# Dilated attention scores: the order of the 128-column and the 32-column matmuls within a visit

## The chip, the cores and the metric

The kernel runs on one core of a Trainium2 chip. The metric is the device time of one execution in microseconds (us), as the median of several runs. TensorE (PE in the profile) multiplies matrices, VectorE is DVE, ScalarE is ACT, GpSimd is POOL, and SyncE (SP) issues most transfers.

## The reference

The program is a trunk of two layers over 512 tokens of width 1024. The first layer mixes tokens by attention in three groups of windows: group 0 is local, group 1 looks at every fourth token, group 2 at every sixteenth. Each group has 16 heads of 64, and the three results are merged by their softmax denominators. The second layer is a gated linear attention. A SwiGLU follows each. Only the scores of the two dilated groups matter here; cut down they are:

```python
A_GROUPS = ((128, 1), (512, 4), (2048, 16))     # window, dilation
half = window // (2 * dilation)
...
scores = jnp.einsum("nbqhd,nbkhd->nbhqk", qp, kb) * (dh ** -0.5)
scores = jnp.where(valid, scores, NEG_INF)
m = jnp.max(scores, axis=-1, keepdims=True)
p = jnp.exp(scores - m)
l = jnp.sum(p, axis=-1)
o = jnp.einsum("nbhqk,nbkhd->nbqhd", p, vb)
```

With 512 tokens, a phase of group 1 has 128 tokens and a phase of group 2 has 32. So 128 queries of one token block need a 128x128 score matrix for group 1, and four 32x32 squares for group 2.

## The kernel before, in words

Nearly all of PE's time goes to projections in split precision: a float32 weight is split into a high and a low part (`wh` by ACT at L107, `wl` by DVE at L108), the activations as well, and three matmuls of 512 columns stand for one product. In the attention layer `chunk_of` (L639) makes these projections; its three matmuls are L658, L659 and L660, and they write the PSUM tiles `ppp`.

`attend_dilated(u)` (L826) does the two dilated groups for four heads (u is 0 to 3): a chunk of keys, one of values, one of queries, and then four **visits**. A visit takes one pair of heads (`pr`) and two of the four token blocks (`i0`, `i0+1`). It has these steps:

- Scores on PE, in float32. Each head of the pair (`a` is 0 or 1) has its own PSUM tile, `pss[a]`, named `ps` in the profile; a block `b` takes 160 columns of it. Columns 0 to 127 are group 1, one matmul of 64 rows by 128 columns per head and block (L851). Columns 128 to 159 are group 2, four matmuls of 64 rows by 32 columns (L856), here called the pieces. Head 0 lies in rows 0 to 63 of the array and head 1 in rows 64 to 127; a piece writes only 32 partitions, so it uses a quarter of the columns. A float32 matmul stands twice in the trace, as two passes, each with its own weight load: 256 pieces in the program are 512 records.
- Softmax (L738): on DVE a masked minimum for each head and block (L748, tile `sm`), on ACT the exponential (L749).
- Turning (L752): four transposes on PE (L757), a copy by ACT (L782), and for the pieces DVE transposes and a spread (L785, L787).
- Weighing (L797): PE multiplies the turned weights with the values into `po`. It is held back by one visit (`self.pending`): the weights of visit n are used behind the transposes of visit n+1.

There are 4 times 4 visits. A scheduler places their instructions among the projections of the chunk that follows, so that between the scores of a visit and its transposes PE works on L658 to L660. Each engine then runs its own instructions in that fixed order. The two score tiles of a visit reuse the two PSUM buffers of the visit before (`"s": 2` in `PBUFS`), which are free once ACT has copied them (L782). In the second visit of u = 0 the scheduler placed the first matmuls of the two heads apart, as the order below shows. After the dilated visits, from about 380 us on, come the local visits with scores in L891.

Of the kernel before, what the change touches and what calls it, by code (L numbers as in the profile page):

```python
# [4 lines left out]

# [1 line left out]

# [15 lines left out]
P = 128  # L23
# [5 lines left out]
HD = 64  # L29
# [12 lines left out]
class Trunk:  # L42
# [300 lines left out]
    def product(self, acc, x, w, width, start, apart=False):  # L343
        mm = self.nc.tensor.matmul
        per = 1024 // width
        last = KT // 2 - 1
        def high(i, k, wh):
            f = slice(k % per * width, (k % per + 1) * width)
            for x_part, first in zip(x[k], (start and k == 0, False)):
                mm(acc[i][:, 0:width], lhsT=x_part[:, i * P:(i + 1) * P], rhs=wh[:, f], start=first, stop=False,  # L350
                   skip_group_check=True)

        def low(i, k, wl):
            f = slice(k % per * width, (k % per + 1) * width)
            self.multiplied = mm(acc[i][:, 0:width], lhsT=x[k][0][:, i * P:(i + 1) * P], rhs=wl[:, f], start=False,  # L355
                                 stop=k == last, skip_group_check=True)

        for n, (wh, wl) in enumerate(w):
            ks = range(n * per, n * per + per)
            for group in ((0,), (1,)) if apart or n == len(w) - 1 else ((0, 1),):  # L360
                for i in group:
                    for k in ks:
                        high(i, k, wh)
                for i in group:
                    for k in ks:
                        low(i, k, wl)
# [459 lines left out]
    def attend_dilated(self, u):  # L826
        nc = self.nc
        k = self.qk_chunk("k", u)
        v = self.v_chunk(self.ins["a_w_v"][u], 0)
        q1, q = self.qk_chunk("q", u)  # L830
        st = self.t("st", (P, NT, 2, 4))
        o_dram = []

        def store(pr, po):
            ob = self.t("ob", (P, 4, 4, 32))
            nc.vector.transpose(ob.rearrange("q r p j -> q p r j"), po.rearrange("q (p r s) -> q p r s", p=4, r=4))
            od = self.dr.tile([S * P], F32, name=f"o_dram_{u}_{pr}")
            for a in range(4):
                nc.gpsimd.dma_start(od.rearrange("(s t a d) -> a s t d", s=32, a=4, d=32)[a],
                                    ob[32 * a:32 * a + 32].rearrange("s r p j -> s (r p) j"))  # L840
            o_dram.append(od)

        for pr in range(2):
            for i0 in (0, 2):
                pss = [self.p("s") for _ in range(2)]
                for b in range(2):
                    i = i0 + b
                    tok = slice(i * P, (i + 1) * P)
                    for a in range(2):
                        r = slice(a * HD, (a + 1) * HD)  # L850
                        nc.tensor.matmul(pss[a][:, b * 160:b * 160 + P], lhsT=q1[pr][r, tok], rhs=k[r, pr, :, i],  # L851
                                         start=True, stop=True)
                    for g in range(4):
                        for a in range(2):
                            r = slice(a * HD, (a + 1) * HD)
                            nc.tensor.matmul(pss[a][32 * g:32 * g + 32, b * 160 + P:b * 160 + 160],  # L856
                                             lhsT=q[r, 2 + pr, g, i], rhs=k[r, 2 + pr, g, i], start=True, stop=True)
                sms = []
                for a in range(2):
                    stats = [[st[:, i0 + b, s, 2 * pr + a:2 * pr + a + 1] for s in range(2)] for b in range(2)]  # L860
                    sms.append(self.softmax(pss[a], [(0, 160)] * 2, 160, self.masks[:, 0:160], stats))
                pts = self.turned(pss, sms, 2, 160, self.finish_dilated)
                vals = lambda i, c, f: v[i][:, c * 256 + f:c * 256 + f + HD]
                self.pending = pts, vals, pr * P, i0, partial(store, pr) if i0 == 2 else None
        std = self.dr.tile([S * 8], F32, name=f"st_dram_{u}")
        for r in range(4):
            nc.gpsimd.dma_start(std.rearrange("(s r c) -> r s c", r=4, c=32)[r],
                                st[32 * r:32 * r + 32].rearrange("p a b c -> p (a b c)"))
        return o_dram, std
# [499 lines left out]
```

## Time and profile before

| what | value |
|---|---|
| median of 3 runs | 1441.89 us (1441.7 to 1441.99) |
| the profiled execution, its own time | 1441.3 us |
| its span in the profile | 1439.5 us |
| PE busy | 1434.3 us (100%) |
| DVE busy | 1019.7 us (71%) |
| ACT busy | 745.8 us (52%) |
| granted clock of PE over the run | 1.0 |

A row of the timeline has the start in us from the span's start, the length in us, the engine, the line of the kernel, the operation, the tiles written and read, the shape, the number of merged records, and in brackets the idle time before it with what ended it. The length of a merged row goes from the first record's start to the last one's end. PE records overlap, because a matmul starts in the array while the one before still drains, so PE is measured here by the time from one start to the next start.

### The profile page before, as it was taken

Reading aid. Unit: us, or ns where it says so; the run is one execution under the profiler, and the core shown is the slowest. Engines: PE = TensorE matmul, PEld = TensorE weight load, DVE = VectorE, ACT = ScalarE, POOL = GpSimd, SP = SyncE. Lnnn points to the kernel's source line nnn. Section 1 sums busy time; section 2 is a strip of 40 time slices with the busy share of each in tenths; the row PEclk is TensorE's granted clock in tenths of the full one; section 3 lists DMA queues with packets and bytes.
Section 4 is the critical chain, followed back from the end, with each engine's and each line's share of the span. In section 5 each row is a group of like instructions: output and inputs, shape, how many; then the busy total and the mean of one; then the engine's idle time right before and its main releaser. Section 6 shows DMA issues by size and latency. Waiting matters only on the chain.

```text
span 1439.5 us, 21062 instructions
## 1 busy us (share of the span) xinstructions
PE 1434.3 (100%) x7766; PEld 1191.0 (83%) x7766; DVE 1019.7 (71%) x1862; ACT 745.8 (52%) x1274; POOL 170.6 (12%) x270
## 2 busy tenths in 40 slices
PE   9999999999999999999999999999999999999999
PEld 8887878787888888888888887888888888889887
DVE  6685868778689669887786335757576987779322
ACT  6444444545456647655575224555744755557211
POOL 0001020101322212211130000000010222221000
PEclk9999999999999999999999999999999999999999
DMA  8544344464543438777785333212155887776542
GB/s 276 140 132 110 104 119 118 101 189 107 132 137 103 122 113 235 194 215 221 230 211 183 122 114 105 88 45 88 56 172 168 231 222 215 214 188 187 169 129 70
DMA packets 96104, 218.57 MB, mean 152 GB/s; under 512 B 15200, under 2 KB 38560, under 8 KB 96000
## 3 DMA queue, kind: packets, MB, share of 16 engines
q1 hardware_dynamic: 78768, 164.62, 35.6%
q0 software_dynamic: 17088, 52.58, 16.6%
q8 instruction: 61, 1.00, 0.3%
q14 instruction: 43, 0.35, 0.1%
q10 hardware_dynamic: 144, 0.02, 0.0%
HBM read 184.59 MB, written 19.99 MB: 142 GB/s over the span
## 4 chain that ended last, share of the span: by engine, by line
PE 94%; DVE 4%; ACT 1%; issue 1%; DMA 0%; DVEq 0%; SPq 0%
PE ppp L121 19%; PE ppp L350 14%; PE ppp L123 10%; PE ppp L660 9%; PE ppp L659 9%; PE ppp L658 9%; PE ppp L355 7%; PE ps L350 6%; PE ps L355 3%; PE po L797 2%; PE ps L851 1%; PE ps L757 1%; PE ppp L1195 1%; PE ps L891 1%; ACT sm L749 1%
## 5 line engine op out<-in xcount | busy, mean ns | idle before, releaser
L107 ACT ACTIVATE wh<-wf 128x1024 fp32r<-128x1024 f32 (+1 forms) x200 | 208.2, 1042 | 325.6 <-PE ppp L121 185.0
L108 DVE TENSOR_TENSOR wl<-wf,wh 128x1024 fp32r<-128x1024 f32 (+1 forms) x200 | 239.3, 1197 | 184.5 <-ACT wh L107 184.1
L658 PE MATMUL ppp<-wh,xs 128*128 128x512 f32 (+1 forms) x668 | 255.3, 382 | 0.0
L660 PE MATMUL ppp<-wh,xs 128*128 128x512 f32 (+1 forms) x668 | 254.5, 381 | 0.0
L659 PE MATMUL ppp<-wl,xs 128*128 128x512 f32 (+1 forms) x668 | 254.3, 381 | 0.0
L121 PE MATMUL ppp<-xs,wh 128*128 128x512 f32 x544 | 170.3, 393 | 0.0
L658 PEld LDWEIGHTS ppp<-wh,xs 128*128 128x128 f32 x668 | 125.6, 188 | 26.9 <-issue 3.4
L660 PEld LDWEIGHTS ppp<-wh,xs 128*128 128x128 f32 x668 | 125.6, 188 | 24.0 <-issue 0.3
L659 PEld LDWEIGHTS ppp<-wl,xs 128*128 128x128 f32 x668 | 125.6, 188 | 23.7 <-issue 0.2
L107 ACT ACTIVATE wh<-wA 128x1024 fp32r<-128x1024 f32 x88 | 93.3, 1061 | 98.1 <-PE ppp L350 37.7
L350 PE MATMUL ppp<-wh,a 128*128 128x512 f32 (+1 forms) x576 | 139.4, 373 | 0.0
L121 PEld LDWEIGHTS ppp<-xs,wh 128*128 128x128 f32 x544 | 101.4, 188 | 23.4 <-issue 1.5
L108 DVE TENSOR_TENSOR wl<-wA,wh 128x1024 fp32r<-128x1024 f32 x88 | 107.3, 1219 | 16.6 <-ACT wh L107 16.6
L350 PEld LDWEIGHTS ppp<-wh,a 128*128 128x128 f32 x576 | 102.1, 188 | 20.0 <-ACT g L415 1.5
L123 PE MATMUL ppp<-xs,wl 128*128 128x512 f32 x272 | 106.0, 390 | 0.0
L749 ACT ACTIVATE sm<-sm,st 128x160 f32<-128x160 f32 (+2 forms) x128 | 56.8, 446 | 45.4 <-DVE st L748 45.2
L355 PE MATMUL ppp<-wl,a 128*128 128x512 f32 (+1 forms) x288 | 78.4, 371 | 0.0
L269 POOL DMA_DIRECT2D wA<-in_gate_up_dram x44 | 38.5, 882 | 312.6 <-DVE wl L108 256.7
L350 PE MATMUL ps<-wh,sh 128*128 128x512 f32 (+1 forms) x192 | 70.3, 371 | 0.0
L350 PE MATMUL ps<-wh,sl 128*128 128x512 f32 (+1 forms) x192 | 70.3, 371 | 0.0
L350 PE MATMUL ppp<-wh,sh 128*128 128x512 f32 (+1 forms) x192 | 70.3, 371 | 0.0
L350 PE MATMUL ppp<-wh,sl 128*128 128x512 f32 (+1 forms) x192 | 70.3, 371 | 0.0
(317 smaller groups left out, 2619.3 us busy)
## 6 DMA issues: line engine op xcount, KB each, us to landing
wA<-in_gate_up_dram POOLq DMA_DIRECT2D x52, 512.0 KB, 6.0
wf<-in_gate_up_dram SPq DMA_DIRECT2D x40, 512.0 KB, 5.1
wf<-in_down_dram SPq DMA_DIRECT2D x32, 512.0 KB, 3.7
wf<-in_a_w_v_dram SPq DMA_DIRECT2D x20, 512.0 KB, 3.7
turned<-g POOLq DMA_DIRECT2D x80, 128.0 KB, 7.4
zq<-zs SPq DMA_DIRECT2D x152, 64.0 KB, 2.1
wf<-in_a_w_q_dram SPq DMA_DIRECT2D x16, 512.0 KB, 3.8
wf<-in_a_w_qk_dram SPq DMA_DIRECT2D x16, 512.0 KB, 3.9
```

The source lines that it names most:

```text
L107: nc.scalar.activation(hi, src, AF.Copy)
L108: self.low = nc.vector.tensor_sub(lo, src, hi.bitcast(F32))
L121: mm(out, lhsT=wh, rhs=part, start=start and k + n == 0, stop=False)
L123: self.multiplied = mm(out, lhsT=wl, rhs=x[0], start=False, stop=stop and k == len(w) - 1)
L269: self.added = nc.gpsimd.dma_start(raw[tag][i], dram[block, i], accum_op=ALU.add)
L350: mm(acc[i][:, 0:width], lhsT=x_part[:, i * P:(i + 1) * P], rhs=wh[:, f], start=first, stop=False, skip_group_check=True)
L355: self.multiplied = mm(acc[i][:, 0:width], lhsT=x[k][0][:, i * P:(i + 1) * P], rhs=wl[:, f], start=False, stop=k == last, skip_group_check ...
L658: mm(a, lhsT=xh, rhs=wh[:, f], start=k == 0, stop=False)
L659: mm(a, lhsT=xh, rhs=wl[:, f], start=False, stop=False)
L660: self.multiplied = mm(a, lhsT=xl, rhs=wh[:, f], start=False, stop=k == KT - 1)
L749: nc.scalar.activation(sm[:, w], sm[:, w], AF.Exp, bias=n, scale=-1.0, accum_out=l)
L797: self.nc.tensor.matmul(o, lhsT=vals(i0 + b, c, c0 + a * HD), rhs=pts[a][b][c], start=c == 0, stop=c == 1)
```

## The change

In a visit the loops over block, head and piece are taken apart: first the four 128-column matmuls of both blocks, then the sixteen pieces of both blocks. The products, operands, PSUM tiles and columns stay the same. Four lines go, so that L851 becomes L848, L856 becomes L852, and all later lines move up by four.

```diff
-from itertools import chain
+from itertools import chain, product
...
                 pss = [self.p("s") for _ in range(2)]
-                for b in range(2):
-                    i = i0 + b
-                    tok = slice(i * P, (i + 1) * P)
-                    for a in range(2):
-                        r = slice(a * HD, (a + 1) * HD)
-                        nc.tensor.matmul(pss[a][:, b * 160:b * 160 + P], lhsT=q1[pr][r, tok], rhs=k[r, pr, :, i],
-                                         start=True, stop=True)
-                    for g in range(4):
-                        for a in range(2):
-                            r = slice(a * HD, (a + 1) * HD)
-                            nc.tensor.matmul(pss[a][32 * g:32 * g + 32, b * 160 + P:b * 160 + 160],
-                                             lhsT=q[r, 2 + pr, g, i], rhs=k[r, 2 + pr, g, i], start=True, stop=True)
+                for b, a in product(range(2), range(2)):
+                    r, i = slice(a * HD, (a + 1) * HD), i0 + b
+                    nc.tensor.matmul(pss[a][:, b * 160:b * 160 + P], lhsT=q1[pr][r, i * P:(i + 1) * P],
+                                     rhs=k[r, pr, :, i], start=True, stop=True)
+                for b, g, a in product(range(2), range(4), range(2)):
+                    r, i = slice(a * HD, (a + 1) * HD), i0 + b
+                    nc.tensor.matmul(pss[a][32 * g:32 * g + 32, b * 160 + P:b * 160 + 160],
+                                     lhsT=q[r, 2 + pr, g, i], rhs=k[r, 2 + pr, g, i], start=True, stop=True)
```

The order of DVE, ACT, POOL and SP is the same in both programs. On PE, this is the first visit of u = 0 before the change. `ps_787` and `ps_788` are the score tiles of the two heads, `zq_429` holds the keys, `qk_782` the queries of group 1, `zq_765` those of group 2.

```order
L658 MATMUL ppp_1223<-wh_1287,xs_151 128x512
L851 MATMUL ps_787<-zq_429,qk_782 128x128
L851 MATMUL ps_788<-zq_429,qk_782 128x128
L856 MATMUL ps_787<-zq_429,zq_765 32x32
L856 MATMUL ps_788<-zq_429,zq_765 32x32
...
L851 MATMUL ps_787<-zq_429,qk_782 128x128
L851 MATMUL ps_788<-zq_429,qk_782 128x128
```

And the same place after it:

```order
L658 MATMUL ppp_1223<-wh_1287,xs_151 128x512
L848 MATMUL ps_787<-zq_429,qk_782 128x128
L848 MATMUL ps_788<-zq_429,qk_782 128x128
L848 MATMUL ps_787<-zq_429,qk_782 128x128
L848 MATMUL ps_788<-zq_429,qk_782 128x128
L852 MATMUL ps_787<-zq_429,zq_765 32x32
L852 MATMUL ps_788<-zq_429,zq_765 32x32
```

The two 128-column matmuls of the second block moved ahead of the eight pieces of the first; the sixteen pieces now stand in one row, and the projection L659 follows as before. Fifteen of the sixteen visits have this pattern.

The second visit of u = 0 is the other one. On PE before, with `ps_835` and `ps_836` as the tiles of the two heads:

```order
L658 MATMUL ppp_1222<-wh_1317,xs_163 128x512
L851 MATMUL ps_835<-zq_429,qk_782 128x128
L856 MATMUL ps_835<-zq_429,zq_765 32x32
L851 MATMUL ps_836<-zq_429,qk_782 128x128
L856 MATMUL ps_836<-zq_429,zq_765 32x32
```

And after:

```order
L658 MATMUL ppp_1222<-wh_1317,xs_163 128x512
L848 MATMUL ps_835<-zq_429,qk_782 128x128 x2
L848 MATMUL ps_836<-zq_429,qk_782 128x128 x2
L852 MATMUL ps_835<-zq_429,zq_765 32x32
L852 MATMUL ps_836<-zq_429,zq_765 32x32
```

Here one piece of head 0 stood between the 128-column matmuls of the two heads. Now both blocks of head 0 come first, then both of head 1, and all pieces behind them.

## The prediction, on record before the run

> **What bounds the kernel now.** I read the page first, then the waits of PE, then the timeline of PE at the dilated visits, then DVE and ACT at the places where a visit's softmax is late.
>
> ```profile
> span 1439.5 us, 21062 instructions
> PE 1434.3 (100%) x7766; PEld 1191.0 (83%) x7766; DVE 1019.7 (71%) x1862; ACT 745.8 (52%) x1274; POOL 170.6 (12%) x270
> PE 94%; DVE 4%; ACT 1%; issue 1%; DMA 0%; DVEq 0%; SPq 0%
> ```
>
> PE is busy for 1434.3 of 1439.5 us, and the chain that ended last is PE for 94%. All the waits of PE in the whole run are these:
>
> ```profile
> PE ppp L92 <- DVE acc L89: 1.2, 1, 1.2
> PE ppp L651 <- DVE wh L105: 0.5, 1, 0.5
> PE pt L818 <- DVE ob L926: 0.2, 1, 0.2
> ```
>
> So time taken out of PE's row ends the program earlier, as long as no wait grows in its place. The change touches PE alone, at the sixteen dilated visits. This is the first one, in PE's timeline:
>
> ```profile
> 106.44 0.39 PE L658 MATMUL ppp<-wh,xs 128*128 128x512 f32 x1
> 106.76 0.49 PE L851 MATMUL ps<-zq,qk 64*128 64x128 f32 x4
> 107.18 0.29 PE L856 MATMUL ps<-zq,zq 64*32 64x32 f32 x16
> 107.40 0.49 PE L851 MATMUL ps<-zq,qk 64*128 64x128 f32 x4
> 107.83 0.29 PE L856 MATMUL ps<-zq,zq 64*32 64x32 f32 x16
> 108.05 0.50 PE L659 MATMUL ppp<-wl,xs 128*128 128x512 f32 x1
> ```
>
> From start to start a visit is 0.42 + 0.22 + 0.43 + 0.22 = 1.29 us: four phases, and nothing idle between them.
>
> **The change part by part.** *The 128-column phase.* What does one pass cost when passes follow each other, and what does a phase cost for standing alone? The transposes have 128 columns as well, and the local scores have two blocks in one phase, with the same halves of the array:
>
> ```profile
> 110.93 0.60 PE L757 MATMUL ps<-ident,sm 128*128 128x128 f32 x4
> L757 PE MATMUL ps<-ident,sm 128*128 128x128 f32 x64 | 9.7, 274 | 0.0
> 380.40 1.03 PE L891 MATMUL ps<-zq 64*128 64x192 f32 x8
> 381.36 0.50 PE L658 MATMUL ppp<-wh,xs 128*128 128x512 f32 x1
> ```
>
> Four transpose records last 0.60 us, and one lasts 0.274, so their starts lie (0.60 - 0.274) / 3 = 0.109 apart. A phase of L851 is two such passes, since the two heads run side by side: 0.218 us. It takes 0.42, so standing alone costs it 0.20: its first weight load, which nothing covers, and the emptying of the array before the next shape. L891 has two blocks, of 192 and 256 columns. At 0.109 us per 128 columns its four passes are 2 x 0.163 + 2 x 0.218 = 0.76 us; with 0.20 once that is 0.96, with 0.20 for each block 1.16. The row says 381.36 - 380.40 = 0.96. So blocks of one shape in a row pay the 0.20 once. Merged, the phase is 0.42 + 0.22 = 0.64 us where two took 0.85: 0.20 saved.
>
> *The piece phase.* How long one piece lasts is in the records of that line:
>
> ```profile
> L856 PE MATMUL ps<-zq,zq x512: 192/203/213, 107.2 to 359.1; 64*32 64x32 f32 x171
> ```
>
> The sixteen records (eight pieces, two passes) last 0.29 us, the last of them 0.192, so the last starts 0.10 behind the first: 0.0066 us each, 0.106 for sixteen. The phase takes 0.22, so 0.116 is the cost of standing alone. Merged it is 0.22 + 0.106 = 0.328 us instead of 0.44: 0.116 saved, if sixteen more starts go as fast as the first sixteen. At worst they pay as much as a phase by itself or more; that is the second and third rival. The Trainium skill ("TensorE: Matmul & The Clock Gate", the section "Wait — 56ns, not 53.3ns?") states that start-to-start never falls below about 25 ns, however few the columns. The 6.6 ns here, where eight tiles of the array work side by side, do not agree with it; by that rule the sixteen added starts would take 0.40 us and the piece phase 0.62.
>
> An ordinary visit so goes from 1.29 to 0.64 + 0.33 = 0.97 us, 0.32 saved, and fifteen of them save 4.8 us.
>
> *The odd visit*, the second of u = 0:
>
> ```profile
> 112.16 0.48 PE L851 MATMUL ps<-zq,qk 64*128 64x128 f32 x2
> 112.57 0.24 PE L856 MATMUL ps<-zq,zq 64*32 64x32 f32 x2
> 112.75 0.48 PE L851 MATMUL ps<-zq,qk 64*128 64x128 f32 x2
> 113.16 0.28 PE L856 MATMUL ps<-zq,zq 64*32 64x32 f32 x14
> 113.38 0.49 PE L851 MATMUL ps<-zq,qk 64*128 64x128 f32 x4
> 114.02 0.50 PE L659 MATMUL ppp<-wl,xs 128*128 128x512 f32 x1
> ```
>
> It has six phases and takes 114.02 - 112.16 = 1.86 us. With two phases it is 0.97, and 0.89 is saved, if the two heads still run side by side although head 1 now stands behind both blocks of head 0. If not, four more passes of 0.109 follow each other, it takes 1.41, and 0.45 is saved. I take 0.89: the lone piece above lasts 0.24, so its second pass starts 0.05 behind its first, yet sixteen records start within 0.10. PE must therefore be starting other tiles while one waits for its second pass.
>
> PE's row gets shorter by 4.8 + 0.89 = 5.7 us.
>
> *What is given back.* Nothing on DVE, ACT, POOL or SP is added or moved, and no queue is passed; transfers are issued behind the same instructions. Scores of both heads are complete at the end of the visit in either order, so the softmax starts no later than now in relation to PE. But where DVE is late for its own reasons, the softmax does not come earlier by the visit's own 0.32 us, while the transposes do. The fourth visit of u = 1 shows it:
>
> ```profile
> 196.28 0.32 DVE L748 CUSTOM_DVE_ANT_0 sm<-ps,masks 128x160 f32<-128x160 f32 x1 [0.16 <-PE ps L856]
> 201.60 0.29 PE L856 MATMUL ps<-zq,zq 64*32 64x32 f32 x16
> 202.73 0.32 DVE L748 CUSTOM_DVE_ANT_0 sm<-ps,masks 128x160 f32<-128x160 f32 x1
> 204.73 0.19 ACT L749 ACTIVATION_READ_ACCUMULATOR sm<-sm,st 128x1 f32 x1
> 205.38 0.60 PE L757 MATMUL ps<-ident,sm 128*128 128x128 f32 x4
> ```
>
> PE's scores end at 201.89, DVE turns to them at 202.73, ACT is through at 204.92, and the transposes start at 205.38: 0.46 us to spare. DVE last waited for PE at 196.28, by 0.16. If DVE's work since the first visit of the group moves by 0.32 + 0.16 = 0.48 only, and PE by four visits, 1.28, then 1.28 - 0.48 - 0.46 = 0.34 us come back as a wait. The fourth visits of u = 0 and u = 2 have less to spare:
>
> ```profile
> 124.51 0.72 DVE L836 STREAM_TRANSPOSE ob<-po 128x512 f32<-128x512 f32 x1 [0.53 <-PE po L797]
> 128.25 0.19 ACT L749 ACTIVATION_READ_ACCUMULATOR sm<-sm,st 128x1 f32 x1
> 128.55 0.49 PE L757 MATMUL ps<-ident,sm 128*128 128x128 f32 x3
> 283.10 0.47 PEld L757 LDWEIGHTS ps<-ident,sm 128*128 128x128 f32 x4 [0.15 <-ACT sm L749]
> ```
>
> In the first DVE waited for PE just ahead of the visit (0.53 at 124.51), so only the visit's own 0.32 counts, against 128.55 - 128.44 = 0.11 to spare: some 0.2 us back. In the second the weight load already waits 0.15 for ACT: up to 0.3 back. At u = 3 a low weight part comes close:
>
> ```profile
> 352.44 1.22 DVE L108 TENSOR_TENSOR wl<-wf,wh 128x1024 fp32r<-128x1024 f32 x1
> 353.96 0.39 PE L659 MATMUL ppp<-wl,xs 128*128 128x512 f32 x1
> ```
>
> It is done at 353.66 and needed at 353.96, 0.30 to spare against 0.32: 0.1 back there, with other small ones. The sum is 0.34 + 0.2 + 0.3 + 0.2 for the rest, about 1.1 us; from both sides it is 0 (all of DVE moves with PE) and, if DVE stood still over each group, up to the first rival's 4.7. I take 1.1, because the waits above are seen. Behind the groups DVE has room, so nothing adds up:
>
> ```profile
> DVE wl L108 <- ACT wh L107: 10.2, 2, 5.9
> ```
>
> This is DVE's wait between 363 and 380 us, 10.2 us of it, ahead of the local visits.
>
> The sum: 5.7 - 1.1 = 4.6 us. The profiled execution took 1441.3 us, 1.8 more than its span, and would take 1436.7. The median of the runs shown is 0.6 above it, 1441.9, so I forecast 1437.3 us. About 0.2% (2.9 us) is what a measurement of this kernel can tell from no change.
>
> **Rivals.** *First: the softmax does not come along.* DVE and ACT stay where they are within each group of four visits, and the transposes wait. To spare are 0.1, 0.46, 0.1 and 0.05 us or so, against 1.85, 1.28, 1.28 and 0.96, so 1.75 + 0.8 + 1.2 + 0.9 = 4.7 of the 5.7 us would come back, and the time is 1440.9. For it: DVE is late in the fourth visits. Against it: DVE's brackets above show it waiting for PE in every group, so its work starts earlier as well. A chance of 0.08 for most of this.
>
> *Second: the pieces are fed slowly.* How many matmuls stand ready for PE when the phase begins? The semaphore waits of PE's sequencer tell where it is:
>
> ```profile
> L851 PEldq EVENT_SEMAPHORE  x2: 51/51/51, 104.4 to 104.5; - x2
> L856 PEldq EVENT_SEMAPHORE  x4: 51/51/51, 104.7 to 105.0; - x4
> L856 PEldq EVENT_SEMAPHORE  x2: 51/51/51, 106.8 to 107.0; - x2
> ```
>
> Each of the first eight pieces of this visit has one such wait. When the scores begin at 106.76, the sequencer is at the seventh: it runs ahead by two L851 and six pieces, about eight matmuls, and stops there until some leave. Before the change eight pieces are a whole phase. Now, of sixteen, eight must be fed while the others run. Call the time to feed one f. The phase is then 8 f + 0.05 for the last second pass + 0.12 to the next phase, 8 f + 0.17, as soon as that is over 0.328. From the rows: four pieces with their waits take 0.1 each (104.7 to 105.0), and two waits with nothing between them are 0.1 apart too (104.4 to 104.5), which leaves a piece nearly nothing; so I take f at 0.02 and the phase at 0.33. At most f is 0.09: by 107.93 the sequencer has delivered ten more matmuls (two L851, eight pieces) since 107.0. If f is 0.05, two starts of 25 ns, the phase takes 0.57 and a visit 1.21 instead of 1.29; sixteen save 1.3, with the odd visit's further 0.57 some 1.8 us, and the time is 1440.1, no change that can be told. This is also what the Trainium skill's floor would make of the pieces that are not queued. A chance of 0.11.
>
> *Third, on the other side: they are fed at the upper bound.* With f = 0.09 the piece phase takes 0.89 and a visit 1.53 instead of 1.29: sixteen lose 3.9, the odd visit gives 0.6 back, and the time is 1445.2. It turns at f = 0.06, where 0.64 + 8 f + 0.17 is 1.29. For it: nothing before the change has more than eight pieces in a row. Against it: the row at 104.4 to 105.0. A chance of 0.05.
>
> *Fourth: the merged phase still empties between blocks*, and the change does nothing: 1441.9. L891 speaks against it. A chance of 0.04.
>
> **How the numbers follow.** My forecast, from 1436.0 (nothing given back, 1441.9 - 5.7, rounded) to about 1438.9 (0.45 for the odd visit, 2.3 given back), has 0.72. The rest of the range up to 1440.0 holds milder forms of the first two rivals. Left out are the end of the second, the third, the fourth and the full first: 0.2. So the range is 1436.0 to 1440.0. Faster by over 0.2%, below 1439.0: 0.72 and a few hundredths of mild forms, 0.75. Within 0.2%: 0.20. Slower: 0.05.
>
> **What would show it.** In the changed profile a visit should have two phases: L848 x8 with 0.64 us to the first L852, and L852 x32 with 0.33 to the next line; the odd visit too. Records of L852 that start further apart in the second half than in the first would show the second or third rival. New waits of PE at L757 for ACT `sm` L749, in the fourth visits above all, would show what is given back. The prediction is wrong if the L848 phase takes 0.85, if the L852 phase takes over 0.5, or if PE's waits in the four groups add up to over 2.5 us.

## The result, and the profile after

The changed kernel takes 1436.85 us, the median of 5 runs (1436.51 to 1436.94); the kernel before took 1441.89 us in 5 runs (1441.7 to 1442.41). The ratio is 0.9964, with a 95% interval of 0.9951 to 0.9976: 5.0 us less, where 4.6 were forecast (1437.3 us, range 1436.0 to 1440.0). The profiled execution took 1436.52 us. Its page:

```profile
span 1434.7 us, 21062 instructions
PE 1429.4 (100%) x7766; PEld 1188.2 (83%) x7766; DVE 1018.6 (71%) x1862; ACT 746.0 (52%) x1274; POOL 170.9 (12%) x270
```

The span is 4.8 us shorter, PE's busy time 4.9 and that of its weight loads (PEld) 2.8; no other engine's changed by more than about 1 us. All the waits of PE that the trace lists:

```profile
PE ppp L92 <- DVE acc L89: 1.2, 1, 1.2
PE ppp L659 <- DVE wl L108: 0.2, 1, 0.2
PE pt L818 <- DVE ob L922: 0.2, 1, 0.2
PE ppp L651 <- DVE wh L105: 0.2, 1, 0.2
```

Only the second is new, and it has nothing to do with the visits: it ends at 8.58 us, at the program's start. Between 100 and 400 us the list has no wait at all. The first visit in PE's timeline, and then the second one, the odd one before the change:

```profile
107.40 0.71 PE L848 MATMUL ps<-zq,qk 64*128 64x128 f32 x8
108.05 0.36 PE L852 MATMUL ps<-zq,zq 64*32 64x32 f32 x32
108.33 0.50 PE L659 MATMUL ppp<-wl,xs 128*128 128x512 f32 x1
...
112.41 0.72 PE L848 MATMUL ps<-zq,qk 64*128 64x128 f32 x8
113.06 0.35 PE L852 MATMUL ps<-zq,zq 64*32 64x32 f32 x32
113.34 0.50 PE L659 MATMUL ppp<-wl,xs 128*128 128x512 f32 x1
```

From start to start a visit is now 0.65 + 0.28 = 0.93 us where it was 1.29, and the odd visit is 0.93 where it was 1.86. All sixteen visits have two phases; one of them, the fourth of u = 1, takes 0.98 because its first phase is 0.69 long. To see what became of that time over the whole stretch, compare the projection that follows the last visit, in PE's timeline of before and then of after:

```profile
359.20 0.50 PE L660 MATMUL ppp<-wh,xs 128*128 128x512 f32 x1
```

```profile
354.43 0.50 PE L660 MATMUL ppp<-wh,xs 128*128 128x512 f32 x1
```

From the start of the first visit to the end of the last it was 359.20 - 106.76 = 252.44 us and is 354.43 - 107.40 = 247.03: 5.41 less. Added over the sixteen visits, the time from the first score matmul to the next other line fell from 21.16 to 14.93 us, 6.23 less. So 0.82 us came back as waits between the visits. Behind the last visit nothing changed: 1439.5 - 359.20 = 1080.3 before, 1434.7 - 354.43 = 1080.3 after. The first visit starts 0.64 us later in this profile; that lies ahead of all that the change touches, and nearly all of it arises at the wait that ends at 8.58 us: L658 ahead of it starts at 7.84 us before and 7.85 after, L660 behind it at 8.30 and 8.92. In the profiles of the experiments that leave the first visit where it was, it starts between 107.2 and 108.0 us. So the difference of the two spans is 5.41 - 0.64 = 4.8 us.

Where did the 0.82 us come back? Normally a transpose starts 0.23 us behind the start of the projection ahead of it. In the fourth visits it does not; here are those of u = 0, 1 and 2 in PE's timeline, then the low weight part of u = 3:

```profile
127.01 0.39 PE L659 MATMUL ppp<-wl,xs 128*128 128x512 f32 x1
127.52 0.65 PE L757 MATMUL ps<-ident,sm 128*128 128x128 f32 x4
...
202.72 0.39 PE L659 MATMUL ppp<-wl,xs 128*128 128x512 f32 x1
203.10 0.44 PE L757 MATMUL ps<-ident,sm 128*128 128x128 f32 x2
...
279.27 0.39 PE L660 MATMUL ppp<-wh,xs 128*128 128x512 f32 x1
279.74 0.44 PE L757 MATMUL ps<-ident,sm 128*128 128x128 f32 x2
...
349.19 0.40 PE L658 MATMUL ppp<-wh,xs 128*128 128x512 f32 x1
349.54 0.50 PE L659 MATMUL ppp<-wl,xs 128*128 128x512 f32 x1
349.88 0.40 PE L660 MATMUL ppp<-wh,xs 128*128 128x512 f32 x1
```

The starts lie 0.51, 0.38 and 0.47 apart, so 0.28, 0.15 and 0.24 us are lost; at u = 3, behind the third visit, it is twice about 0.11, where L659 starts late, at 349.54, just behind the end of a low weight part on DVE (349.49). That makes 0.9 us. Against it, the transposes of one visit of u = 3 were 0.07 late before the change and no longer are, which leaves the 0.82 within 0.02. PE's list of waits does not name any of these; the times from start to start show them. Why the softmax is late shows on DVE at the fourth visit of u = 0:

```profile
124.18 1.18 DVE L108 TENSOR_TENSOR wl<-wf,wh 128x1024 fp32r<-128x1024 f32 x1
125.28 0.31 DVE L748 CUSTOM_DVE_ANT_0 sm<-ps,masks 128x160 f32<-128x160 f32 x1
```

The visit's scores started at 123.41 and are complete at 124.41, but DVE is inside a low weight part and turns to them at 125.28.

### The profile page after: what moved, and what is told of

Read it like the earlier page. It is cut to its first block, busy times and chain, and to the rows that moved or that the text cites. A ratio compares the mean times of both kernels' runs of the same rounds, so it can differ in the third digit from the quotient of the medians.

```text
span 1434.7 us, 21062 instructions
## 1 busy us (share of the span) xinstructions
PE 1429.4 (100%) x7766; PEld 1188.2 (83%) x7766; DVE 1018.6 (71%) x1862; ACT 746.0 (52%) x1274; POOL 170.9 (12%) x270
## 4 chain that ended last, share of the span: by engine, by line
PE 91%; DVE 6%; ACT 2%; issue 1%; DMA 0%; SPq 0%; DVEq 0%; ACTq 0%
PE ppp L121 19%; PE ppp L350 14%; PE ppp L123 10%; PE ppp L660 8%; PE ppp L659 8%; PE ppp L658 8%; PE ppp L355 7%; PE ps L350 6%; PE ps L355 3%; PE po L797 1%; ACT sm L749 1%; DVE wl L108 1%; PE ps L757 1%; PE ppp L1191 1%; DVE sm L748 1%
## 5 line engine op out<-in xcount | busy, mean ns | idle before, releaser
L108 DVE TENSOR_TENSOR wl<-wf,wh 128x1024 fp32r<-128x1024 f32 (+1 forms) x200 | 239.2, 1197 | 188.8 <-ACT wh L107 188.4
L658 PE MATMUL ppp<-wh,xs 128*128 128x512 f32 (+1 forms) x668 | 255.7, 383 | 0.0
L659 PE MATMUL ppp<-wl,xs 128*128 128x512 f32 (+1 forms) x668 | 254.7, 381 | 0.2 <-DVE wl L108 0.2
L660 PE MATMUL ppp<-wh,xs 128*128 128x512 f32 (+1 forms) x668 | 254.8, 381 | 0.0
L658 PEld LDWEIGHTS ppp<-wh,xs 128*128 128x128 f32 x668 | 125.7, 188 | 27.0 <-issue 3.3
L659 PEld LDWEIGHTS ppp<-wl,xs 128*128 128x128 f32 x668 | 125.7, 188 | 24.3 <-DVE wl L108 0.9
L660 PEld LDWEIGHTS ppp<-wh,xs 128*128 128x128 f32 x668 | 125.7, 188 | 23.9 <-issue 0.3
L108 DVE TENSOR_TENSOR wl<-wA,wh 128x1024 fp32r<-128x1024 f32 x88 | 107.4, 1220 | 16.6 <-ACT wh L107 16.6
```

The lines of the kernel that those rows point to most:

```text
L108: self.low = nc.vector.tensor_sub(lo, src, hi.bitcast(F32))
L658: mm(a, lhsT=xh, rhs=wh[:, f], start=k == 0, stop=False)
L659: mm(a, lhsT=xh, rhs=wl[:, f], start=False, stop=False)
L660: self.multiplied = mm(a, lhsT=xl, rhs=wh[:, f], start=False, stop=k == KT - 1)
```

## The experiments

The theory was: (1) what is saved is the cost of a change of shape, about 0.20 us for each 128-column phase and 0.16 for each piece phase (0.222 alone, of which 0.063 stay when it is merged), so the number of phases sets the visit's time, and the order within them does not matter; (2) sixteen pieces go in a row without being fed slowly; (3) what is given back comes from DVE's low weight part ahead of the fourth visits' softmax. The rivals were that the heads' adjacency or the place of a phase counts, that the pieces run dry, and that the waits come from elsewhere. Five of the kernels split a visit into two functions, and differ in one line:

```diff
+                def wide(b):
+                    for a in range(2):
+                        ...
+                def pieces(b):
+                    for g, a in product(range(4), range(2)):
+                        ...
+                for step, b in (...):
+                    step(b)
```

### Only the 128-column phases merged

```diff
+                for step, b in ((pieces, 0), (wide, 0), (wide, 1), (pieces, 1)):
```

> Order of a visit: pieces of block 0, the 128-column matmuls of both blocks, pieces of block 1 (three phases instead of before's four; the second visit of u = 0 has five). Theory (each phase pays once for its first weight load and for the emptying of the array): an ordinary visit takes 0.222 + 0.645 + 0.222 = 1.09 us instead of 1.29, 15 visits save 3.0 us, the odd one some 0.4, about 0.5 comes back in waits: about 1439.0 us (1438.4 to 1439.8), and the middle phase is 0.645 long. Rival (what counts is that the 128-column matmuls stand ahead of all pieces, for the softmax behind them): the gain is gone, about 1442.

Measured: 1451.49 us (1451.32 to 1451.74), ratio 1.0066 [1.0053, 1.008]. The visit came out as expected and the total did not. An ordinary visit:

```profile
120.85 0.29 PE L855 MATMUL ps<-zq,zq 64*32 64x32 f32 x16
121.07 0.71 PE L849 MATMUL ps<-zq,qk 64*128 64x128 f32 x8
121.72 0.29 PE L855 MATMUL ps<-zq,zq 64*32 64x32 f32 x16
121.94 0.50 PE L660 MATMUL ppp<-wh,xs 128*128 128x512 f32 x1
```

That is 0.22 + 0.65 + 0.22 = 1.09 us: the merged 128-column phase costs the same here, between two piece phases, as in the changed kernel. The total is lost elsewhere. Since the pieces now stand first, the scheduler places the first visit's pieces one by one between projections, eight in each of the four groups. One of them:

```profile
98.53 0.40 PE L658 MATMUL ppp<-wh,xs 128*128 128x512 f32 x1
98.86 0.24 PE L855 MATMUL ps<-zq,zq 64*32 64x32 f32 x2
99.03 0.50 PE L659 MATMUL ppp<-wl,xs 128*128 128x512 f32 x1
99.38 0.40 PE L660 MATMUL ppp<-wh,xs 128*128 128x512 f32 x1
```

From 98.53 to 99.38 it is 0.85 us, where two projections take 0.46: one lone piece costs 0.39 us. Thirty-two of them are 12.5, less 0.9 for the four piece phases that they replace and 3.2 for the merged phases: 8.4 of the 9.7 us that this kernel is slower; the rest was not traced. The odd visit was expected to save 0.4 and saves 0.2: it has five phases and takes 1.67 us. The visits' phases decide on the theory here, the total does not.

### Only the piece phases merged

```diff
+                for step, b in ((wide, 0), (pieces, 0), (pieces, 1), (wide, 1)):
```

> Order of a visit: 128-column matmuls of block 0, the sixteen pieces of both blocks, 128-column matmuls of block 1 (three phases in all sixteen visits). Theory (cost per phase): a visit takes 0.422 + 0.285 + 0.422 = 1.13 us instead of 1.29, 15 visits save 2.4 us, the odd one 0.7, about 0.5 comes back: about 1439.3 us (1438.6 to 1440.0). Rival (the 128-column matmuls must stand first): about 1442.

Measured: 1441.92 us (1441.49 to 1442.74), ratio 1.0 [0.9991, 1.001], beside 1441.76 of before. Again the phases are as expected. An ordinary visit, and then a projection at 317 us:

```profile
118.38 0.49 PE L849 MATMUL ps<-zq,qk 64*128 64x128 f32 x4
118.81 0.35 PE L855 MATMUL ps<-zq,zq 64*32 64x32 f32 x32
119.09 0.49 PE L849 MATMUL ps<-zq,qk 64*128 64x128 f32 x4
119.51 0.50 PE L660 MATMUL ppp<-wh,xs 128*128 128x512 f32 x1
...
317.12 0.50 PE L658 MATMUL ppp<-wh,xs 128*128 128x512 f32 x1 [1.18 <-ACT xs L151]
```

Three phases take 0.43 + 0.28 + 0.42 = 1.13 us, and the merged piece phase costs the same 0.28 between two 128-column phases. Over all visits this takes 2.6 us out of PE's row, although the first phases of three visits are some 0.5 us longer. Yet the time did not fall. The reordered scores led the scheduler to another order on DVE, ACT and SP, and with it came the wait of 1.18 us for ACT at 317 us; from start to start PE loses about 2.0 us between 312 and 326 us. From the start of the first visit to the end of the last it is 252.14 us, 0.3 less than before; this profile also started about 1 us late. So the total says nothing about the phases.

### All pieces first

```diff
+                for step, b in ((pieces, 0), (pieces, 1), (wide, 0), (wide, 1)):
```

> Order of a visit: all sixteen pieces first, then the four 128-column matmuls; in the first visit of each u the scheduler puts the 128-column matmuls between the pieces of the two blocks. Theory (cost per phase): twelve visits have two phases and take 0.93 us as in the changed kernel, four have three and take 1.09, so 0.6 us more than the changed kernel: about 1437.5 us (1436.8 to 1438.2). Rival (the 128-column matmuls must stand first): 1441 or more.

Measured: 1449.98 us (1449.45 to 1450.86), ratio 1.0056 [1.0043, 1.007]. An ordinary visit is two phases with the time of the changed kernel, 0.29 + 0.64 = 0.93 us:

```profile
120.60 0.36 PE L855 MATMUL ps<-zq,zq 64*32 64x32 f32 x32
120.89 0.72 PE L849 MATMUL ps<-zq,qk 64*128 64x128 f32 x8
121.53 0.50 PE L660 MATMUL ppp<-wh,xs 128*128 128x512 f32 x1
```

Which shape comes first makes no difference to such a visit; eight of the twelve visits behind the groups' first ones are like it, three take 1.00 and one 1.07 us, with a longer piece phase whose cause was not traced. The total was missed mainly for the reason of the first experiment: in the first visits of all four groups, where three phases were expected, the pieces stand between projections, six alone and two groups of five. How much of the 8.2 us they explain was not added up.

### Four phases, with the blocks exchanged

```diff
+                for step, b in ((wide, 1), (pieces, 1), (wide, 0), (pieces, 0)):
```

> Four phases in another order: 128-column matmuls and pieces of block 1, then those of block 0. The order on DVE, ACT, POOL and SP is that of the changed kernel. Theory (only the number of phases counts): 0.42, 0.22, 0.42 and 0.22 us, as before the change; with the odd visit at 1.29 instead of 1.86 about 1441.3 us (1440.8 to 1441.9). Rival (which block comes last counts, for the softmax): over 0.2% away from that.

Measured: 1442.21 us (1442.08 to 1442.72) beside 1442.12 of before, ratio 1.0001 [0.9991, 1.001]. The other engines keep their order in this kernel, so here the total can serve: four phases stay four phases, and nothing is gained.

```profile
119.52 0.49 PE L849 MATMUL ps<-zq,qk 64*128 64x128 f32 x4
119.94 0.29 PE L855 MATMUL ps<-zq,zq 64*32 64x32 f32 x16
120.16 0.49 PE L849 MATMUL ps<-zq,qk 64*128 64x128 f32 x4
120.58 0.29 PE L855 MATMUL ps<-zq,zq 64*32 64x32 f32 x16
```

The expectation was wrong in one point: the odd visit was to become an ordinary one of 1.29 us. The scheduler kept its six phases, and it takes 1.86 us as before.

### Head 1 behind both blocks of head 0, in every visit

```diff
-                for b, a in product(range(2), range(2)):
+                for a, b in product(range(2), range(2)):
                     r, i = slice(a * HD, (a + 1) * HD), i0 + b
```

> The changed kernel, with the 128-column matmuls of both blocks of head 0 first, then those of head 1, in all visits as the odd one has it. Order elsewhere unchanged. Theory (the two halves of the array run side by side also when one head's matmuls stand behind the other's): 0.65 us for the phase, +0.1 us in all, about 1436.9 us (1436.5 to 1437.4). Rival (head 1 waits for head 0): 1.08 us for the phase, 6.5 us more, about 1443.4 us.

Measured: 1436.76 us (1436.48 to 1436.82), ratio 0.9963 [0.9949, 0.9977].

```profile
117.84 0.72 PE L848 MATMUL ps<-zq,qk 64*128 64x128 f32 x8
118.49 0.35 PE L852 MATMUL ps<-zq,zq 64*32 64x32 f32 x32
```

The phase takes 0.65 us, as in the odd visit of the changed kernel. Its eight records start in four pairs, 0.013 us apart within a pair. So the two heads run side by side whether or not they alternate in the row, and that fits only if PE starts head 1's first matmul, the third in the row, ahead of head 0's second. Were they one after the other, four passes of 0.109 would be added, 0.44 us for each visit.

### The pieces computed twice

In the order wide 0, wide 1 and then the pieces of both blocks two times over, this kernel computes all pieces twice, into the same places.

```diff
+                for step, b in ((wide, 0), (wide, 1), (pieces, 0), (pieces, 1), (pieces, 0), (pieces, 1)):
```

> The changed kernel, with the sixteen pieces of a visit computed twice, one set behind the other: 32 pieces in a row. Sixteen took 0.285 us, of which the second eight cost 0.063. Theory (feeding does not bind): 0.285 + 2 x 0.063 = 0.41 us for the phase. Rival (eight or so wait ready, the rest is fed at 0.02 to 0.09 us each, which sixteen don't show): 0.6 us or more, and starts further apart in the second half. The whole time is of no use here, since the scheduler orders the other engines anew.

Measured in one profile (1442.7 us, a single execution): the piece phase takes 120.07 - 119.38 = 0.69 us, not 0.41.

```profile
119.38 0.76 PE L855 MATMUL ps<-zq,zq 64*32 64x32 f32 x64
120.07 0.50 PE L660 MATMUL ppp<-wh,xs 128*128 128x512 f32 x1
```

The records' starts tell where. In the same timeline, cut off at 119.6, the group holds 32 records within 0.35 us:

```profile
119.38 0.35 PE L855 MATMUL ps<-zq,zq 64*32 64x32 f32 x32
```

These are the sixteen pieces of the first round, their last start 0.16 us behind the first, as in the changed kernel. Then no matmul starts for 0.08 us, and the second round settles at 0.017 us a piece (two pieces, four records, every 0.033 us). All sixteen visits show the same steps. So a slower regime exists behind the sixteenth piece; the change uses exactly sixteen. Is it slow feeding, as the second rival had it? A piece is two weight loads and two matmuls, so sixteen are 64 instructions; the Trainium skill ("TensorE: Matmul & The Clock Gate", the table at its beginning) gives 64 as the depth of PE's queue, and the trace agrees with that in where the burst ends. It does not prove it: the second round also writes again what the first wrote, and a wait for that would begin at the same piece. PE's weight loads speak against feeding as the cause of the gap. The last one that runs ahead of the gap is the thirty-third, the seventeenth piece's first:

```profile
119.51 0.11 PEld L855 LDWEIGHTS ps<-zq,zq 64*32 64x32 f32 x1
```

It starts 0.13 us behind the first matmul, right behind the loads of the first round, so the seventeenth piece had reached PE before the gap. Its matmul starts only at 119.62, when this load ends, 0.11 us behind the load's start; in the first round a matmul follows the start of its load by 0.035 us at most. What the seventeenth piece waits for, and what sets the 0.017 us behind it, stays open.

### The softmax placed earlier

The call of the softmax in a dilated visit is given a higher priority in the scheduler.

```diff
+                    with self.tc.high_priority(offset=AHEAD):
+                        sms.append(self.softmax(pss[a], [(0, 160)] * 2, 160, self.masks[:, 0:160], stats))
```

> The changed kernel, with the softmax of the dilated visits ahead of other work of DVE and ACT (as the local visits have it). PE's order is the same. Theory (about 0.8 us comes back at the transposes, because the softmax of late visits stands behind a low weight part on DVE): those waits go, up to 0.8 us less, about 1436.2 us (1435.8 to 1436.7). Rival (the low weight parts are as late as the softmax, and the wait only moves to them): 1436.9 or up to 1 us more.

Measured: 1436.69 us (1436.22 to 1436.86), ratio 0.9963 [0.995, 0.9975], which is the changed kernel's time. It decides nothing. DVE's order changed only in a few places from 267 us on, the low weight part stayed ahead of L748 in all four fourth visits, and the wait at u = 0 stayed (0.52 us from start to start at 127.21). At u = 1 this execution shows no wait, with an unchanged order there; at u = 2 it is 0.21, and 0.08 and 0.12 appear at two transposes that had none.

### The stored tile's transpose behind the softmax

At the fourth visits the DVE transpose L836 of the finished output is held until the softmax has been issued.

```diff
+            if then and hold and c0 == 0:
+                self.due = partial(then, self.po)
...
+                    with self.tc.issue_after(self.reduced.ins):
+                        due()
```

> The changed kernel, with one DVE instruction per u moved: the transpose of the finished output tile (tile ob, 0.72 us), which stands ahead of the softmax of the fourth visit, goes behind it. On PE the transposes of that visit come one to three projection matmuls earlier. Theory (what is given back are the waits of the transposes for the late softmax in the fourth visits, 0.29, 0.16 and 0.24 us in the changed profile): they go, and the time is 0.7 us less than that of the changed kernel, about 1436.2 us (1435.8 to 1436.6). Rival (something else ends those waits, such as the low weight parts on DVE or ACT's own work): they stay, and the time is 1436.9.

Measured: 1437.33 us (1436.83 to 1437.77), ratio 0.9967 [0.9955, 0.998] beside 1442.12 of before. The waits were expected to go, and they did not. DVE at the fourth visit of u = 0:

```profile
124.50 1.23 DVE L108 TENSOR_TENSOR wl<-wf,wh 128x1024 fp32r<-128x1024 f32 x1 [0.28 <-ACT wh L107]
125.64 0.32 DVE L748 CUSTOM_DVE_ANT_0 sm<-ps,masks 128x160 f32<-128x160 f32 x1
```

With the 0.71 us of L836 gone, DVE waits 0.28 us for ACT's high weight part, and L108 still stands ahead of L748. The transposes start 0.51 us behind the projection ahead of them, as without the edit; at u = 1, 2 and 3 it is 0.51, 0.49 and 0.67, no less than without it. So L836 is not the cause. Of what the rival names, L108 still stands ahead of the softmax, and ACT's exponentials behind it.

### The low weight part behind the softmax

The one low weight part that stands ahead of a fourth visit's softmax is put behind it, for the first three groups. To tell a gain of this size, the changed kernel was run again on the same chip.

```diff
-        self.low = nc.vector.tensor_sub(lo, src, hi.bitcast(F32))
+        with self.tc.issue_after(self.behind.ins) if self.behind else nullcontext():
+            self.low = nc.vector.tensor_sub(lo, src, hi.bitcast(F32))
...
+            self.behind = self.reduced if self.late_low and kk == 2 else None
             wh, wl = ready[kk] if ready else self.weight(dram[kk], 1024)
```

> The changed kernel, with three DVE instructions moved: for u = 0, 1 and 2 the low weight part (L108, 1.2 us) that stands ahead of the softmax of the fourth visit goes behind it. On PE the transposes of that visit come two, five and two projection matmuls earlier (0.46, 1.1 and 0.46 us). Theory (that low part holds the softmax back, and so causes the waits of 0.29, 0.16 and 0.24 us): the softmax of the fourth visits starts about 0.8 us earlier, right behind the scores, the waits of u = 0 and u = 2 go, that of u = 1 may stay, and the time is 0.5 to 0.7 us below that of the changed kernel in the same call. Rival (the waits come from ACT's exponentials or from elsewhere): the waits stay where they are, and the time is that of the changed kernel or more.

> The changed kernel once more, to be compared with the other run of this call: 1436.9 us (1436.5 to 1437.3); nothing in it tells the theories apart.

Measured: 1435.98 us (1435.76 to 1436.34), ratio 0.996 [0.9946, 0.9973], and for the changed kernel again 1436.72 us (1436.29 to 1436.87), ratio 0.9964 [0.9951, 0.9976]. On DVE and on PE with the edit (L108 is L111 here, the other lines shown are 5 to 7 higher), then the changed kernel again:

```profile
124.48 0.32 DVE L753 CUSTOM_DVE_ANT_0 sm<-ps,masks 128x160 f32<-128x160 f32 x1 [0.31 <-PE ps L859]
...
125.46 1.22 DVE L111 TENSOR_TENSOR wl<-wf,wh 128x1024 fp32r<-128x1024 f32 x1
```

```profile
126.45 0.40 PE L665 MATMUL ppp<-wh,xs 128*128 128x512 f32 x1
126.72 0.66 PE L762 MATMUL ps<-ident,sm 128*128 128x128 f32 x4
```

```profile
127.06 0.39 PE L659 MATMUL ppp<-wl,xs 128*128 128x512 f32 x1
127.61 0.44 PE L757 MATMUL ps<-ident,sm 128*128 128x128 f32 x2 [0.16 <-ACT sm L749]
```

DVE now waits for PE's scores, as it should where PE is the bound, and turns to the low part afterwards. The transposes start 0.27 us behind the projection instead of 0.55. At u = 2 the wait is gone too. At u = 1 it is 0.16 us with the edit and without: there the transposes moved forward by five matmuls, and now stand right behind ACT's exponentials, which end at 201.57, while the transposes start at 201.62. The edit moved the transposes of u = 0 and u = 2 forward as well, by two matmuls, so it did not change the order of DVE alone; but transposes that come earlier leave the softmax less time, which by itself would make the waits longer. The medians differ by 0.74 us, and the lowest run of the changed kernel lies 0.05 us below the highest here; the ratios' intervals overlap widely. In the rows the waits that went are 0.28 and 0.24, 0.52 us in all, and they carry this point more than the time does. Of all kernels here this has the lowest median.

## Why the prediction was right

**The 128-column phase.** "Merged, the phase is 0.42 + 0.22 = 0.64 us where two took 0.85": it is 0.645 in the ordinary visits. The first experiment showed the same phase alone. The rival that the merged phase still empties between blocks has fallen. What is paid once instead of twice is the change between shapes: four phases in another order gain nothing, two gain 0.36 us a visit in either order, and three gain about half (0.20 or 0.16). The Trainium skill ("TensorEngine Tiling (Array Packing)", the section "Key Properties") states that changing the tiling mode drains TensorE. The phases here agree with that, and give it a price: 0.20 us for a 128-column phase and 0.16 for a piece phase. How that divides between the emptying and the first weight load, no run here separates.

**The piece phase.** The mechanism was right and the size was off. The term "0.0066 us each, 0.106 for sixteen", for the sixteen added starts, was too large. This is the line of the pieces after the change:

```profile
L852 PE MATMUL ps<-zq,zq x512: 192/193/214, 108.0 to 354.3; 64*32 64x32 f32 x171
```

A group of 32 records lasts 0.355 us and the last of them 0.192, so its last start lies 0.163 behind the first, where sixteen records took 0.10. The added sixteen records took 0.063, that is 4 ns each, and the phase is 0.285 us, not 0.328. So merging saved 0.16 us of piece phases, not 0.116. Over sixteen visits that is 0.7 us. The 128-column phases, 0.645 instead of 0.64, took 0.1 of it, and the visits saved 6.2 us where 5.7 were forecast.

**The odd visit.** 0.89 us was forecast to be saved, 0.93 was. The reason given, that PE starts other tiles while one waits for its second pass, fits both this visit and the experiment with the heads apart, which paid 0.007 us a visit.

**What is given back.** Forecast were 0.2, 0.34 and 0.3 us in the fourth visits of u = 0, 1 and 2, and 0.2 for the rest; the profile shows 0.28, 0.15, 0.24 and 0.23. The places were right. The sum was 0.82 instead of 1.1: the forecast's terms add up to 1.04, and at u = 1 DVE moved along further than assumed (its L748 came 0.86 us earlier behind the start of the group, not 0.48). One reading behind the term of u = 2 was wrong: the weight load's wait of 0.15 for ACT cost PE nothing before the change, where those transposes start the normal 0.23 us behind the projection. In the last experiment, with the low weight part behind the softmax, the waits of u = 0 and u = 2 go although the transposes there come earlier, which shows that part as their cause. At u = 1 the wait stayed, then behind ACT's exponentials; at u = 3 it was not tried.

**The rivals.** That the softmax does not come along would have shown 4.7 us of waits, and 0.82 are there. Of the second and third, the step that failed is the reading that PE has "about eight matmuls" ready: sixteen go out in a burst, and no later start among them is slow. The reading came from the semaphore waits at the beginning of the scores; from there, in the changed kernel, four 128-column matmuls and 0.65 us of time still lie ahead of the pieces, which probably is enough to bring the rest up. It did not harm the forecast, since at the value taken for f it gave the same phase; it put some probability on two cases that did not occur.

**The sum.** Forecast was 5.7 - 1.1 = 4.6 us. The profiles show 6.2 - 0.8 = 5.4 between the first visit and the last, the medians 5.0. The two errors, 0.5 and 0.3 us, point the same way, so that the forecast was too small by 0.8 us where the change acts. The rest of the difference is in how single executions differ: the first visit starts 0.64 us later in the profile after the change, and the profiled execution before it was 0.6 us below its median, the one after it 0.3. That the medians come within 0.5 us of the forecast is in part luck.

## What to carry to other kernels

Where one engine is the bound, count its changes of matmul shape, measured from start to start, and not only its work: here two phases fewer saved 0.36 of 1.29 us with the same products. An order written in the code reaches the chip only through the scheduler, so look at every engine's row: two other orders of the same products had shorter visits than before too, and were 0.6 to 0.7% slower in all. Then look for the engine whose own late work now stands ahead of the shortened stage, and move that work behind it.

## What the runs showed of the hardware

- Sixteen 64-row by 32-column float32 matmuls, 32 records, start within 0.163 us, the second half of them 4.5 ns apart; with the same sixteen computed once more behind them there is a gap of 0.08 us and then 0.017 us for each matmul.
- A single such matmul between two 512-column projections costs PE 0.39 us: 0.17 from its start to the next, and 0.1 more for each of the projections around it.
- A phase of four 128-column matmuls, two blocks of two heads, takes the same 0.65 us whether the heads alternate in the row or follow each other.
